# Strassen products in half of an output projection: four weight tiles loaded 20 tiles ahead, their sums formed earlier, one group of products moved

## The chip, the cores and the metric

The kernel runs on one core of a Trainium2 chip. The time is the device time of one launch in microseconds (us), taken from several executions; the profile is one profiled execution. The engines are named PE (TensorE, matrix products; PEld is its weight loading), DVE (VectorE), ACT (ScalarE), POOL (GpSimd) and SP (SyncE, here the engine that issues nearly all DMAs). They run side by side, each works its own instructions strictly in order, and they wait for one another through semaphores.

## The reference

One step of a hybrid encoder layer for two groups of tokens, 256 "prompt" and 32 "sample" tokens, D = 1024, all in float32. The part that matters here is the end:

```python
mixed = sigmoid(ga) * (branch_a @ w_out_a) + sigmoid(gb) * (branch_b @ w_out_b)
return layer_norm(DN_ALPHA * x + mixed @ w_o, ln_g, ln_b)
```

Before it come one big input projection `x @ w_in`, an mLSTM recurrence (branch A, whose final states `C_prompt` are outputs too) and a sparse attention (branch B).

## The kernel before

All weights are cut into 117 tiles of 128 x 1024 numbers (512 KB), worked one after the other in the order of the table `ORDER`. Its end is: `ga` 0 (tile 93), `wa` 0 (94), `ga` 1, `wa` 1, ... `ga` 7 (107), `wa` 7 (108), then the eight tiles of `w_o` (109 to 116; `POS["wo", 0]` is 109). The first five tiles are treated apart, the others run through a loop over the slot `t`.

A float32 product is made of three faster products: each operand is split in a high part (rounded to the type fp32r, an ACT copy, `split_hi`) and the rest (a DVE subtraction, `split_lo`), and high x high, high x low and low x high are summed. `product(t)` is 24 PE instructions for a tile, 3 for each of 8 blocks of 128. In slot `t` the program lists: the load of tile `t + 9` (`load_tile`, an SP DMA into one of eight buffers `wst`), `split_lo(t + 2)` on DVE, `evac(t - 1)` (what DVE, ACT and POOL do with the finished product, which frees one of two banks `pj`), `split_hi(t + 3)` on ACT, then `product(t)` on PE, and in its middle `side()`, where other work booked with `at(slot, ...)` is listed. Nothing orders these but the listing, the queues of the engines and the waits for data and buffers. The split parts have a ring of four buffer pairs, `wh` and `wl`.

The evacuation of a `wa` tile is a chain: DVE multiplies with the gate (`sg`), DVE adds (`mB`), ACT rounds the sum to `mxh`, DVE subtracts (`mxl`); POOL copies sample's 32 tokens to `mxs`. `mxh`/`mxl` are the left operand of `mixed @ w_o`.

The output projection of the 256 prompt tokens is done in `finish()`. Its first four of eight blocks of the summed dimension (512 of 1024) use Strassen's scheme: with `mixed` cut into a11, a12, a21, a22 and the upper half of `w_o` into b11, b12, b21, b22 (one 512 KB tile each, tiles 109 to 112 in this order), seven products replace eight. Token sums s1 to s4 (`token_sums`, `token_halves`) and weight sums t1 to t4 (`weight_sum`, one DVE subtraction of 128 x 1024 each, line L1019) are formed first:

```python
first, second = {"t1": ("b12", "b11"), "t2": ("b22", "t1"), "t3": ("b22", "b12"), "t4": ("b21", "t2")}[name]
dve.tensor_tensor(lazy["sums"][name], raw_unit(first), raw_unit(second), OP.subtract)
```

`seventh(bank, s, t)` issues one such product, a group of six PE instructions of 512 columns (line L1057). `plain(bank, rows, column)` issues a group of twelve for the lower half of `w_o` (tiles 113 to 116, called w4 to w7). `unit_hi`/`unit_lo` split a unit (b.., t.. or w..); w7 and t4 have buffers of their own, `wown` and `spare`. `b11`, `b21` and `t2` are split in the last turns of the loop. The results collect in PSUM banks y11, y12, y21, y22, and y21 is read between its groups: PE adds a11 x b11, DVE takes that to `z` (`begun(0, 0, y21)`, line L1145), PE adds s2 x t2 to the same bank, DVE reads again (`begun(0, 1, y21)`), PE adds s3 x t3, DVE reads again (`added(1, 1, y21)`, line L1149). So each of these PE groups must wait until DVE has read the one before.

Sample's 32 tokens are multiplied with the unsplit weights by `sample_rows(p)` (line L1078; 64 records in the profile), on four 32-column strips of PE side by side; DVE then takes bank `p` to `zs`. At the end come the layer norm on DVE (with a power on POOL), the stores of `y` by SP, and `state_prompt(h)`: 48 PE instructions (`c`), eight ACT copies (`oc_all`) and the stores of `C_prompt`.

Of the kernel before, what the change touches and what calls it, by code (L numbers as in the profile page):

```python
# [14 lines left out]
OP = mybir.AluOpType  # L15
# [8 lines left out]
KT = D // 128  # L24
# [6 lines left out]
FIRST = 5  # L31
SEVEN = ("b11", "b21", "t2", "t1", "t3")
# [6 lines left out]
ALPHA = 2.0 ** 0.25  # L39
# [42 lines left out]
ORDER = tile_order()  # L82
NT = len(ORDER)
POS = {t: i for i, t in enumerate(ORDER)}


def ap_of(t, offset, dims):
# [4 lines left out]
def body(ctx, tc, a, o):  # L92
    nc = tc.nc
    pe, act, dve, pool, sp = nc.tensor, nc.scalar, nc.vector, nc.gpsimd, nc.sync
# [5 lines left out]
    def sb(name, shape, dt=F32, tag=None, bufs=1):  # L100
        return P.tile(shape, dt, name=name, tag=tag or name, bufs=bufs)

    def bank(name, n=512):
        return ps.tile([128, 512], F32, name=name, tag="side", bufs=6)
# [4 lines left out]
    def at(slot, fn, *args):  # L109
        jobs[slot].append((fn, args))  # L110
# [13 lines left out]
    store, lazy, masked = {}, {}, []  # L124
    stage = {}
# [4 lines left out]
    def load_tile(t):  # L130
        if t >= NT or t in loaded:
            return
        loaded.add(t)
        stage[t] = sb(f"wst{t}", [128, KT * 128], tag="wst", bufs=8)
        sp.dma_start(stage[t], a["w"][:, t - FIRST])

    def pair(name):
# [10 lines left out]
    def unit_hi(u, home=None):  # L148
        if home is None:
            home = pair("_" + u)  # L150
        split[u] = home
        act.copy(split[u][0], raw_unit(u))

    def unit_lo(u):
        wh, wl = split[u]
        dve.tensor_tensor(wl, raw_unit(u), wh.bitcast(F32), OP.subtract)  # L156

    def split_hi(t):
        if t >= POS["wo", 0]:
            unit_hi(SEVEN[t - POS["wo", 0]])  # L160
            return
        if t in high:
            return
        load_tile(t)
        split[t] = pair(t)
        act.copy(split[t][0], stage[t])  # L166
        high.add(t)

    def split_lo(t):
        if t >= POS["wo", 0]:  # L170
            unit_lo(SEVEN[t - POS["wo", 0]])
            return
        wh, wl = split[t]
        dve.tensor_tensor(wl, stage[t], wh.bitcast(F32), OP.subtract)  # L174
# [22 lines left out]
    cki = early[:, 1376:1632]  # L197
    early2 = sb("early2", [8, NREL + 40], tag="vaT")
    rtab, rbt = early2[:, 0:NREL], early2[:, NREL:]
    lead = [sb(f"wst_k{k}", [128, KT * 128], tag="wst", bufs=8) for k in range(KT)]  # L200
    cut = T + SMALL
    mid = cut + 256
    sp.dma_start(lead[0][:, 0:cut], a["first"][:, 0, 0:cut])
# [9 lines left out]
    for k in range(KT):  # L213
# [14 lines left out]
        for part, cols in ((whf, slice(0, c)), (wh, slice(c, LEAD - T))):  # L228
            if cols.stop:
                own = slice(T + cols.start, T + cols.stop)  # L230
# [510 lines left out]
    homes = (("hn", "kw"), ("hn", "kw"), ("lg", "lg", "lg", "sw"), ("sw", "ba", "ba", "qs"))  # L741
# [276 lines left out]
        first, second = {"t1": ("b12", "b11"), "t2": ("b22", "t1"), "t3": ("b22", "b12"), "t4": ("b21", "t2")}[name]  # L1018
        dve.tensor_tensor(lazy["sums"][name], raw_unit(first), raw_unit(second), OP.subtract)  # L1019

    at(POS["wo", 0] - 6, token_sums)
    at(POS["wo", 0] - 4, token_halves)
    for n, back in (("t1", 4), ("t2", 2), ("t3", 2), ("t4", 1)):
        at(POS["wo", 0] - back, weight_sum, n)

    def moving(n):
        if n == "wb":
# [31 lines left out]
    def seventh(p, x, u, first=False):  # L1059
        x = standing(x)  # L1060
        w = split.pop(u)
        for k in range(2):
            group(p, [v[:, k] for v in x], w, slice(512 * k, 512 * k + 512), first and k == 0, k == 1)
# [7 lines left out]
    def sample_rows(p):  # L1071
        for k in range(KT):
            for q in range(4):
                if k < 4:
                    w, c = stage[POS["wo", 2 * (k // 2) + q // 2]], 512 * (k % 2) + 256 * (q % 2)
                else:
                    w, c = stage[POS["wo", k]], 256 * q
                pe.matmul(p[32 * q:32 * q + 32, 0:256], lhsT=lazy["mxs"][:, k], rhs=w[:, c:c + 256],  # L1078
                          start=(k == 0), stop=(k == KT - 1))
# [46 lines left out]
            sp.dma_start(lazy[n + "s"], ap_of(a["ln_gb"], D * i, [[256, 4], [0, TS], [1, 256]]))  # L1126

    at(POS["ga", 3], load_tail)
    at(POS["wo", 0] - 1, load_affine)

    def statistics(b, r, records):
        mv = sb(f"mv{b}", [128, 2])
# [6 lines left out]
    def finish():  # L1139
        z, zs, bst, bss = lazy["xn"], lazy["zs"], lazy["bst"], lazy["bss"]  # L1140
        g, be = lazy["g"], lazy["b"]

        def begun(b, c, p):
            half = slice(512 * c, 512 * c + 512)
            dve.scalar_tensor_tensor(z[:, b, half], z[:, b, half], ALPHA, p, op0=OP.mult, op1=OP.add)  # L1145

        def added(b, c, p):
            half = slice(512 * c, 512 * c + 512)
            dve.tensor_tensor(z[:, b, half], z[:, b, half], p, OP.add)  # L1149

        def recorded(b, c):
            dve.bn_stats(bst[:, b, c], z[:, b, 512 * c:512 * c + 512])

        def centred(b):
            mv, nr = statistics(b, slice(0, 128), bst[:, b].rearrange("p a b -> p (a b)"))
            dve.scalar_tensor_tensor(z[:, b], z[:, b], mv[:, 0:1], g, op0=OP.subtract, op1=OP.mult)
            return nr[:, 1:2]

        def scaled(b, rs):
            for c in (slice(0, 512), slice(512, 1024)):  # L1160
                dve.scalar_tensor_tensor(z[:, b, c], z[:, b, c], rs, be[:, c], op0=OP.mult, op1=OP.add)

        def put(c):
            c = slice(512 * c, 512 * c + 512)
            sp.dma_start(o["y"][128:256, c], z[:, 1, c])

        own = sb("wown", [128, 2, KT * 128], F32R, tag="a1")
        spare = sb("spare", [128, 2, KT * 128], F32R, tag="a3")
        lazy["oc"] = sb("oc_all", [128, AH, 2, CROW], tag="a6")
        pool.memset(lazy["oc"][:, :, :, 257:], 0.0)  # L1170
        y11, y12, y21, y22 = (bank(f"yn{i}") for i in range(4))
        p = bank("yns")

        unit_lo("t2")
        evac(POS["wo", 0] - 1, prev)
        seventh(y21, "a11", "b11", True)
        seventh(y11, "a12", "b21", True)
        unit_hi("t1")
        begun(0, 0, y21)
        unit_lo("t1")  # L1180
        seventh(y21, "s2", "t2")
        unit_hi("t3")
        unit_lo("t3")
        sample_rows(p)
        unit_hi("w4")
        begun(0, 1, y21)
        unit_lo("w4")
        unit_hi("w5")
        unit_lo("w5")
        seventh(y12, "s1", "t1", True)  # L1190
        unit_hi("w7", (own[:, 0], own[:, 1]))
        unit_lo("w7")
        seventh(y21, "s3", "t3")
        unit_hi("w6")
        r = slice(96, 128)
        dve.scalar_tensor_tensor(zs, lazy["xs"], ALPHA, p[:, 0:256], op0=OP.mult, op1=OP.add)
        begun(1, 1, y12)
        unit_lo("w6")
        added(1, 1, y21)
        plain(y11, 0, 0)  # L1200
        unit_hi("b22")
        unit_lo("b22")
        dve.bn_stats(bss[:, 3], zs)
        for q in range(3):
            dve.tensor_copy(bss[r, q], bss[32 * q:32 * q + 32, 3])
        mv, nr = statistics(2, r, bss[r].rearrange("p a b -> p (a b)"))
        for q in range(4):
            pool.tensor_copy(nr[32 * q:32 * q + 32, 0:1], mv[r, 0:1])
        for q in range(3):
            pool.tensor_copy(nr[32 * q:32 * q + 32, 1:2], nr[r, 1:2])  # L1210
        unit_hi("t4", (spare[:, 0], spare[:, 1]))
        unit_lo("t4")
        seventh(y12, "s4", "b22")
        plain(y12, 0, 1)
        added(0, 0, y11)
        recorded(0, 0)
        dve.scalar_tensor_tensor(zs, zs, nr[:, 0:1], lazy["gs"], op0=OP.subtract, op1=OP.mult)
        dve.scalar_tensor_tensor(zs, zs, nr[:, 1:2], lazy["bs"], op0=OP.mult, op1=OP.add)
        sp.dma_start(ap_of(o["y"], TP * D, [[256, 4], [D, TS], [1, 256]]), zs)
        seventh(y21, "a22", "t4")  # L1220
        plain(y21, 1, 0)
        plain(y22, 1, 1, True)
        added(0, 1, y12)
        recorded(0, 1)
        rs = centred(0)
        scaled(0, rs)
        sp.dma_start(o["y"][0:128], z[:, 0])
        begun(1, 0, y21)
        recorded(1, 0)
        added(1, 1, y22)  # L1230
        recorded(1, 1)
        rs = centred(1)
        for h in range(AH - 1):
            state_prompt(h)
        scaled(1, rs)
        for c in range(2):
            put(c)
        state_prompt(AH - 1)
# [36 lines left out]
    split_hi(FIRST + 2)  # L1275
    split_lo(FIRST + 2)
    held = {FIRST: (0, 1), FIRST + 1: (2,), FIRST + 2: (3,), FIRST + 3: (4,)}
    for t in range(FIRST, POS["wo", 0]):
        cur[0] = t
        for i in range(FIRST, t + 10):  # L1280
            load_tile(i)
        if FIRST < t <= CALM:
            evac(t - 1, prev)
        for i in held.get(t, ()):
            evac(i, first[i])
        if t < CALM:
            split_hi(t + 3)
        if t > FIRST:
            split_lo(t + 2)
        if t > CALM:  # L1290
            evac(t - 1, prev)
        if t >= CALM:
            split_hi(t + 3)
        prev = product(t, side)
# [88 lines left out]
```

## Time and profile before

| | us |
|---|---|
| median of 3 runs | 417.64 (416.25 to 417.68) |
| the profiled execution, whole | 417.65 |
| its span (first to last instruction) | 415.7 |
| PE busy in the span | 407.7 (98%) |
| DVE busy | 330.2 (79%) |
| ACT busy | 220.6 (53%) |
| POOL busy | 195.1 (47%) |

Times in rows of the profile count from the start of the span. "Busy" of PE has matrix products with modelled ends, which overlap. A row of a timeline gives start, duration, engine, line, operation, output<-operands, and in brackets the idle time before it with what ended that. `yn` stands for y11 to y22, `yns` for sample's bank, `wl_b`, `wl_t`, `wl_w` for low parts of b, t and w units.

### The profile page before, as it was taken

The page shows a single profiled execution, that of the slowest core. Times are in us where ns is not written, and L with a number is a line of the kernel's source. Part 1 is how long each engine was busy: PE and PEld are TensorE (multiplying, and loading weights), DVE is VectorE, ACT ScalarE, POOL GpSimd, SP SyncE. Part 2 cuts the span into 40 slices and gives each one's busy share as a digit, 9 for nine tenths or more (in the row PEclk, how much of TensorE's full clock was granted, in tenths as well). Part 3 has the DMA queues.
Part 4 walks back from the last instruction along what each step waited for, and adds up shares of the span by engine and source line. Part 5 has one row for each costly group of instructions (what it writes and reads, how often), then busy time and mean ns, then how long its engine had stood idle before and what let it go on. Part 6 is the DMA issues. An engine that isn't in the chain of part 4 may idle for free.

```text
span 415.7 us, 8484 instructions
## 1 busy us (share of the span) xinstructions
PE 407.7 (98%) x3111; PEld 395.1 (95%) x3111; DVE 330.2 (79%) x674; ACT 220.6 (53%) x426; POOL 195.1 (47%) x448
## 2 busy tenths in 40 slices
PE   9999999999999999999999999999999999996996
PEld 7999999999999999999989999999999999995686
DVE  5879789996976878797879878997765465979785
ACT  5796564543765556666535565564443354645402
POOL 0200069981397668669500045856998571000041
PEclk9999999999999999999999999999999999999899
DMA  8977889788954854769934755446656558344005
GB/s 298 387 287 212 305 277 308 249 197 273 344 149 137 275 153 134 200 186 168 303 106 118 259 141 153 143 127 182 176 151 183 154 152 309 103 140 140 0 14 208
DMA packets 43151, 81.09 MB, mean 195 GB/s; under 512 B 20682, under 2 KB 25670, under 8 KB 42182
## 3 DMA queue, kind: packets, MB, share of 16 engines
q1 hardware_dynamic: 42390, 79.73, 61.7%
q10 hardware_dynamic: 720, 0.82, 0.5%
q8 instruction: 24, 0.39, 0.4%
q14 instruction: 17, 0.14, 0.1%
HBM read 73.38 MB, written 9.06 MB: 198 GB/s over the span
## 4 chain that ended last, share of the span: by engine, by line
PE 89%; DVE 5%; ACT 2%; issue 1%; DMA 1%; ACTq 0%; DVEq 0%
PE pj L1043 24%; PE pj L1042 24%; PE pj L1044 24%; PE yn L1057 5%; PE pj L1106 1%; DVE wl L174 1%; PE yns L1078 1%; ACT wh L166 1%; DMA wst<-in_w 1%; PE pj L1101 1%; DVE t L1019 1%; PE pj L1099 1%; DVE wl_b L156 1%; DVE mB L993 1%; DVE kx L753 1%
## 5 line engine op out<-in xcount | busy, mean ns | idle before, releaser
L1043 PE MATMUL pj<-xhl,wh 128*128 128x288 f32 x704 | 207.9, 295 | 0.0
L1042 PE MATMUL pj<-xhl,wh 128*128 128x288 f32 x704 | 207.8, 295 | 0.0
L1044 PE MATMUL pj<-xhl,wl 128*128 128x288 f32 x704 | 207.6, 295 | 0.0
L174 DVE TENSOR_TENSOR wl<-wst,wh 128x1024 fp32r<-128x1024 f32 x104 | 129.7, 1248 | 17.6 <-ACT wh L166 17.2
L1042 PEld LDWEIGHTS pj<-xhl,wh 128*128 128x128 f32 x704 | 132.7, 189 | 0.6 <-issue 0.5
L1043 PEld LDWEIGHTS pj<-xhl,wh 128*128 128x128 f32 x704 | 132.6, 188 | 0.0
L1044 PEld LDWEIGHTS pj<-xhl,wl 128*128 128x128 f32 x704 | 132.4, 188 | 0.0
L166 ACT CAST wh<-wst 128x1024 fp32r<-128x1024 f32 x104 | 109.1, 1049 | 10.7 <-PE pj L1043 5.1
L121 POOL COPY pt<-bm 32x96 f32<-32x96 f32 x128 | 48.8, 381 | 19.9 <-DVE bm L636 10.7
L121 POOL COPY kaT<-kn 32x128 f32<-32x128 f32 x64 | 30.1, 471 | 5.1 <-DVE kn L734 2.5
L121 POOL COPY vn<-qaT 32x128 f32<-32x128 f32 x64 | 29.0, 453 | 2.6
L121 POOL COPY hn<-qaT 32x128 f32<-32x128 f32 x32 | 15.5, 485 | 12.1 <-DVE qaT L710 5.6
L994 POOL COPY mxs<-mB 128x32 f32<-128x32 f32 x8 | 1.7, 210 | 38.0 <-DVE mB L993 38.0
L1042 PE MATMUL pj<-bah,wh 128*128 128x288 f32 x64 | 19.0, 297 | 0.3 <-DVE sg L992 0.3
L121 POOL COPY hn<-ht 32x128 f32<-32x128 f32 x32 | 14.7, 459 | 9.3 <-DVE ht L710 8.1
L1044 PE MATMUL pj<-bah,wl 128*128 128x288 f32 x64 | 18.9, 296 | 0.0
L1043 PE MATMUL pj<-bal,wh 128*128 128x288 f32 x64 | 18.9, 296 | 0.0
L1042 PE MATMUL pj<-bbh,wh 128*128 128x288 f32 x64 | 18.9, 295 | 0.0
L1043 PE MATMUL pj<-bbl,wh 128*128 128x288 f32 x64 | 18.9, 295 | 0.0
L1044 PE MATMUL pj<-bbh,wl 128*128 128x288 f32 x64 | 18.9, 295 | 0.0
L979 ACT ACTIVATE sg<-pj 128x288 f32<-128x288 f32 x16 | 6.5, 408 | 22.1 <-PE pj L1044 22.1
L912 ACT CAST mxh<-mB 128x288 fp32r<-128x288 f32 x8 | 3.5, 433 | 25.5 <-DVE mB L993 25.5
(510 smaller groups left out, 687.0 us busy)
## 6 DMA issues: line engine op xcount, KB each, us to landing
wst<-in_w SPq DMA_DIRECT2D x112, 512.0 KB, 4.3
wst_k<-in_first SPq DMA_DIRECT2D x5, 440.0 KB, 6.7
rscr<-rrow SPq DMA_DIRECT2D x2, 768.0 KB
out_k<-kbT SPq DMA_DIRECT2D x1, 1152.0 KB, 10.1
vrows<-vat SPq DMA_DIRECT2D x8, 144.0 KB, 1.8
stC<-in_state_C SPq DMA_DIRECT2D x1, 1028.0 KB
out_C_sample<-stC SPq DMA_DIRECT2D x1, 1028.0 KB
bm<-rscr SPq DMA_DIRECT2D x1, 1024.0 KB
```

The lines of the kernel that those rows point to most:

```text
L121: pool.tensor_copy(out(quads[k], quads[i]), turned(quads[i], quads[k]))
L156: dve.tensor_tensor(wl, raw_unit(u), wh.bitcast(F32), OP.subtract)
L166: act.copy(split[t][0], stage[t])
L174: dve.tensor_tensor(wl, stage[t], wh.bitcast(F32), OP.subtract)
L753: dve.scalar_tensor_tensor(kwl[b], k, gnat[:, b, 2, h:h + 1], kwh[b].bitcast(F32), op0=OP.mult, op1=OP.subtract)
L979: act.activation(sg, q, AF.Sigmoid)
L993: dve.tensor_tensor(mx, sg, mx, OP.add)
L1019: dve.tensor_tensor(lazy["sums"][name], raw_unit(first), raw_unit(second), OP.subtract)
L1042: pe.matmul(p[:, :T], lhsT=wh[:, c], rhs=h[:, k], start=(k == 0), stop=False)
L1043: pe.matmul(p[:, :T], lhsT=wh[:, c], rhs=l[:, k], start=False, stop=False)
L1044: pe.matmul(p[:, :T], lhsT=wl[:, c], rhs=h[:, k], start=False, stop=(k == KT - 1))
L1057: pe.matmul(p, lhsT=l, rhs=r, start=first and i == 0, stop=last and i == 2, skip_group_check=True)
```

## The change

The buffers `wst` are no longer one ring of eight: `load_plan` writes out for each slot which tile is loaded and into which of eight homes. Up to tile 97 nothing is different. In slots 89 to 92 the tiles 109 to 112 (b11, b12, b21, b22) are loaded, where 98 to 101 were; they keep four of the homes. Tiles 98 to 108 and 113 to 116 follow in slots 93 to 107 through the four other homes. The four weight sums are listed in slots 94, 96, 98 and 100 in place of 105, 107, 107 and 108. In `finish()` sample's products stand ahead of s2 x t2, and the splits and reads are listed in another order.

```diff
+WO = POS["wo", 0]
+EARLY = WO - 20
+
+def load_plan():
+    slots, homes = defaultdict(list), {}
+    for t in range(FIRST, EARLY + 9):
+        slots[max(t - 9, FIRST)].append(t)
+        homes[t] = (t - FIRST) % 8
+    for i in range(4):
+        slots[EARLY + i].append(WO + i)
+        homes[WO + i] = (EARLY + 9 + i - FIRST) % 8
+    rest = [*range(EARLY + 9, WO), *range(WO + 4, NT)]
+    for i, t in enumerate(rest):
+        slots[EARLY + 4 + i].append(t)
+        homes[t] = (EARLY + 13 + i % 4 - FIRST) % 8
+    return slots, homes
...
-        stage[t] = sb(f"wst{t}", [128, KT * 128], tag="wst", bufs=8)
+        stage[t] = sb(f"wst{t}", [128, KT * 128], tag=f"wst{HOMES[t]}")
...
-    for n, back in (("t1", 4), ("t2", 2), ("t3", 2), ("t4", 1)):
-        at(POS["wo", 0] - back, weight_sum, n)
+    for i, n in enumerate(("t1", "t2", "t3", "t4")):
+        at(EARLY + 5 + 2 * i, weight_sum, n)
...
         begun(0, 0, y21)
         unit_lo("t1")
-        seventh(y21, "s2", "t2")
+        sample_rows(p)
         unit_hi("t3")
         unit_lo("t3")
-        sample_rows(p)
         unit_hi("w4")
+        unit_lo("w4")
+        unit_hi("w7", (own[:, 0], own[:, 1]))
+        unit_lo("w7")
+        seventh(y21, "s2", "t2")
+        dve.scalar_tensor_tensor(zs, lazy["xs"], ALPHA, p[:, 0:256], op0=OP.mult, op1=OP.add)
+        dve.bn_stats(bss[:, 3], zs)
         begun(0, 1, y21)
-        unit_lo("w4")
         unit_hi("w5")
         unit_lo("w5")
         seventh(y12, "s1", "t1", True)
-        unit_hi("w7", (own[:, 0], own[:, 1]))
-        unit_lo("w7")
+        begun(1, 1, y12)
+        unit_hi("w6")
+        unit_lo("w6")
         seventh(y21, "s3", "t3")
-        unit_hi("w6")
-        r = slice(96, 128)
-        dve.scalar_tensor_tensor(zs, lazy["xs"], ALPHA, p[:, 0:256], op0=OP.mult, op1=OP.add)
-        begun(1, 1, y12)
-        unit_lo("w6")
+        unit_hi("b22")
+        unit_lo("b22")
         added(1, 1, y21)
         plain(y11, 0, 0)
-        unit_hi("b22")
-        unit_lo("b22")
-        dve.bn_stats(bss[:, 3], zs)
+        unit_hi("t4", (spare[:, 0], spare[:, 1]))
+        unit_lo("t4")
...
-        unit_hi("t4", (spare[:, 0], spare[:, 1]))
-        unit_lo("t4")
...
-        for i in range(FIRST, t + 10):
+        for i in LOADS[t]:
             load_tile(i)
```

DVE from slot 105 to the split of t2, before (`sums` is the low part of the token sums, `t_5193` holds t1 to t3, `t_5194` is t4):

```order
L1010 TENSOR_TENSOR sums<-sq,sums 128x1024
L1019 TENSOR_TENSOR t_5193<-wst_4996,wst_4963 128x1024
L174 TENSOR_TENSOR wl_5175<-wst_4921,wh_5174 128x1024
L156 TENSOR_TENSOR wl_b_5214<-wst_4963,wh_b_5213 128x1024
L992 TENSOR_TENSOR sg_5211<-pj_5216,sg_5211 128x288
L993 TENSOR_TENSOR mB<-sg_5211,mB 128x288
L913 TENSOR_TENSOR mxl<-mB,mxh 128x288
L1019 TENSOR_TENSOR t_5193<-wst_5077,t_5193 128x1024
L1019 TENSOR_TENSOR t_5193<-wst_5077,wst_4996 128x1024
L156 TENSOR_TENSOR wl_b_5250<-wst_5038,wh_b_5249 128x1024
L1019 TENSOR_TENSOR t_5194<-wst_5038,t_5193 128x1024
L156 TENSOR_TENSOR wl_t_5283<-t_5193,wh_t_5282 128x1024
```

The same stretch of DVE now (the lines are those of the changed file, 20 higher):

```order
L1030 TENSOR_TENSOR sums<-sq,sums 128x1024
L194 TENSOR_TENSOR wl_5181<-wst_5083,wh_5180 128x1024
L176 TENSOR_TENSOR wl_b_5217<-wst_4539,wh_b_5216 128x1024
L1012 TENSOR_TENSOR sg_5214<-pj_5219,sg_5214 128x288
L1013 TENSOR_TENSOR mB<-sg_5214,mB 128x288
L933 TENSOR_TENSOR mxl<-mB,mxh 128x288
L176 TENSOR_TENSOR wl_b_5253<-wst_4612,wh_b_5252 128x1024
L176 TENSOR_TENSOR wl_t_5284<-t_4745,wh_t_5283 128x1024
```

All four sums have left this stretch. They stand now in the slots of `wa` tiles, here t2 and t3 in slots 96 and 98 on DVE:

```order
L1039 TENSOR_TENSOR t_4745<-wst_4651,t_4745 128x1024
L194 TENSOR_TENSOR wl_4816<-wst_4724,wh_4815 128x1024
L1012 TENSOR_TENSOR sg_4813<-pj_4818,sg_4813 128x288
L1013 TENSOR_TENSOR mB<-sg_4813,mB 128x288
L933 TENSOR_TENSOR mxl<-mB,mxh 128x288
L194 TENSOR_TENSOR wl_4857<-wst_4764,wh_4856 128x1024
L1039 TENSOR_TENSOR t_4745<-wst_4651,wst_4575 128x1024
L194 TENSOR_TENSOR wl_4894<-wst_4810,wh_4893 128x1024
```

Each sum came between the two weight splits of a pair of tiles.

On PE in `finish()`, around the end of sample's products, now (`yn_5321` is y21, `yn_5320` is y12):

```order
L1098 MATMUL yns<-wst_5211,mxs 32x256 x4
L1098 MATMUL yns<-wst_5244,mxs 32x256 x4
L1077 MATMUL yn_5321<-wh_t_5283,sums 128x512
L1077 MATMUL yn_5321<-wl_t_5284,sums 128x512
L1077 MATMUL yn_5321<-wh_t_5283,sums 128x512 x2
```

Before, the same place on PE went on with y12, since s2 x t2 stood ahead:

```order
L1078 MATMUL yns<-wst_5208,mxs 32x256 x4
L1078 MATMUL yns<-wst_5241,mxs 32x256 x4
L1057 MATMUL yn_5320<-wh_t_5342,sums 128x512
L1057 MATMUL yn_5320<-wl_t_5343,sums 128x512
L1057 MATMUL yn_5320<-wh_t_5342,sums 128x512 x2
```

Sample's products now stand between a12 x b21 and s2 x t2.

More of the change, by code (lines that the diff above doesn't have):

```diff
@@ L84 @@
 POS = {t: i for i, t in enumerate(ORDER)}
+WO = POS["wo", 0]
[13 more added lines that the diff above has]
+    return slots, homes
+LOADS, HOMES = load_plan()
 def ap_of(t, offset, dims):
@@ L158, in split_hi @@
     def split_hi(t):
-        if t >= POS["wo", 0]:
-            unit_hi(SEVEN[t - POS["wo", 0]])
+        if t >= WO:
+            unit_hi(SEVEN[t - WO])
             return
@@ L169, in split_lo @@
     def split_lo(t):
-        if t >= POS["wo", 0]:
-            unit_lo(SEVEN[t - POS["wo", 0]])
+        if t >= WO:
+            unit_lo(SEVEN[t - WO])
             return
@@ L199, in body @@
     rtab, rbt = early2[:, 0:NREL], early2[:, NREL:]
-    lead = [sb(f"wst_k{k}", [128, KT * 128], tag="wst", bufs=8) for k in range(KT)]
+    lead = [sb(f"wst_k{k}", [128, KT * 128], tag=f"wst{k}") for k in range(KT)]
     cut = T + SMALL
@@ L1019, in weight_sum @@
         dve.tensor_tensor(lazy["sums"][name], raw_unit(first), raw_unit(second), OP.subtract)
-    at(POS["wo", 0] - 6, token_sums)
-    at(POS["wo", 0] - 4, token_halves)
-    for n, back in (("t1", 4), ("t2", 2), ("t3", 2), ("t4", 1)):
-        at(POS["wo", 0] - back, weight_sum, n)
+    at(WO - 6, token_sums)
+    at(WO - 4, token_halves)
+    for i, n in enumerate(("t1", "t2", "t3", "t4")):
+        at(EARLY + 5 + 2 * i, weight_sum, n)
     def moving(n):
@@ L1128, in body @@
     at(POS["ga", 3], load_tail)
-    at(POS["wo", 0] - 1, load_affine)
+    at(WO - 1, load_affine)
     def statistics(b, r, records):
@@ L1172, in finish @@
         p = bank("yns")
+        r = slice(96, 128)
         unit_lo("t2")
-        evac(POS["wo", 0] - 1, prev)
+        evac(WO - 1, prev)
         seventh(y21, "a11", "b11", True)
@@ L1277, in body @@
     held = {FIRST: (0, 1), FIRST + 1: (2,), FIRST + 2: (3,), FIRST + 3: (4,)}
-    for t in range(FIRST, POS["wo", 0]):
+    for t in range(FIRST, WO):
         cur[0] = t
-        for i in range(FIRST, t + 10):
+        for i in LOADS[t]:
             load_tile(i)
```

## The prediction

> **What bounds the kernel now.** I read the page's first lines, then the waits of TensorE (PE), then the timelines of PE and VectorE (DVE) at the end, and last the granted clock in the place where PE had stood.
>
> The page: span, and busy time of PE with its share and number of instructions.
>
> ```profile
> span 415.7 us, 8484 instructions
> PE 407.7 (98%) x3111; PEld 395.1 (95%) x3111; DVE 330.2 (79%) x674; ACT 220.6 (53%) x426; POOL 195.1 (47%) x448
> ```
>
> PE is the engine to save time on. The span is 415.7 us and the execution took 417.65, so 1.95 us lie around it; the median of the runs is 417.64, so I use this execution's own time. The waits of PE from 340 us on are two (total, times, longest):
>
> ```profile
> PE yn L1057 <- DVE xn L1145: 3.3, 1, 3.3
> PE pj L1042 <- DVE sg L992: 0.3, 1, 0.3
> ```
>
> The PE timeline around them (start, duration, line, output<-operands, idle time before it):
>
> ```profile
> 372.97 0.40 PE L1042 MATMUL pj<-bah,wh 128*128 128x288 f32 x1 [0.27 <-DVE sg L992]
> 376.12 0.30 PE L1044 MATMUL pj<-bah,wl 128*128 128x288 f32 x1
> 376.25 0.40 PE L1057 MATMUL yn<-wh_b,mxh 128*128 128x512 f32 x1
> 378.87 0.39 PE L1057 MATMUL yn<-wh_b,mxl 128*128 128x512 f32 x1
> 382.61 0.47 PE L1057 MATMUL yn<-wh_t,sums 128*128 128x512 f32 x1 [3.35 <-DVE xn L1145]
> 384.35 5.11 PE L1078 MATMUL yns<-wst,mxs 128*32 128x256 f32 x64
> 389.39 0.49 PE L1057 MATMUL yn<-wh_t,sums 128*128 128x512 f32 x1
> 406.21 0.28 PE L766 MATMUL c<-v1h,kx 128*128 128x258 f32 x1
> ```
>
> The last tile of products ends at 376.25, two groups of six follow, and then PE stands 3.35 us until DVE has read bank y21 (`begun(0, 0, y21)`, L1145). Why DVE is late there, its own timeline shows:
>
> ```profile
> 369.06 1.22 DVE L1019 TENSOR_TENSOR t<-wst,wst 128x1024 f32<-128x1024 f32 x1
> 374.29 1.22 DVE L1019 TENSOR_TENSOR t<-wst,t 128x1024 f32<-128x1024 f32 x1
> 375.42 1.22 DVE L1019 TENSOR_TENSOR t<-wst,wst 128x1024 f32<-128x1024 f32 x1
> 376.56 1.22 DVE L156 TENSOR_TENSOR wl_b<-wst,wh_b 128x1024 fp32r<-128x1024 f32 x1
> 377.69 1.22 DVE L1019 TENSOR_TENSOR t<-wst,t 128x1024 f32<-128x1024 f32 x1
> 379.96 0.45 DVE L992 TENSOR_TENSOR sg<-pj,sg 128x288 f32<-128x288 f32 x1
> 381.78 0.68 DVE L1145 SCALAR_TENSOR_TENSOR xn<-xn,yn 128x512 f32<-128x512 f32 x1
> ```
>
> The four weight sums (L1019) stand in one unbroken queue ahead of the last tile's evacuation (L992 at 379.96, though its product ended 3.4 us earlier). From one such instruction's start to the next is 1.13 to 1.14 us (375.42 to 376.56), so they take 4 x 1.135 = 4.54 us. The stall has a second price: the stretches of sample's products (columns: PE busy with count, weight loads, DVE, granted clock, DMA share, GB/s).
>
> ```profile
> 384.34:387.34 3.00, 2.99 (x29) 1.39 (x33) 0.00 (x0) 0.50 0.00 0
> 387.34:389.39 2.05, 2.05 (x40) 0.96 (x32) 0.00 (x0) 1.00 0.00 0
> ```
>
> After the hole the granted clock is 0.50 until 387.3. The 64 recorded products go four side by side, 16 steps: 7 steps of 0.427 us at half clock, then 9 in 2.05 us, 0.228 each.
>
> The Trainium skill, TensorE: Matmul & The Clock Gate, Part 1 ("What's actually happening"), has the clock halve after an idle window of about 3.4 us that runs freely, so that a hole of 3.35 us need not always fill one. The one trace has the drop; a run of the kernel before that escapes it would be 1.7 us shorter (417.65 - 1.7 = 415.95), near the shortest of the three times, 416.25. By the row the new kernel gains against 417.65 on every run; by the rule it gains up to 1.7 less against such runs, and its own time is the same by both.
>
> **The change, part by part.**
>
> *Sums moved to slots 94, 96, 98, 100.* Four DVE instructions, 1.14 us each, now stand ahead of the second weight split (L174) of those tiles' turn. There DVE waits on ScalarE (ACT):
>
> ```profile
> 329.55 1.23 DVE L174 TENSOR_TENSOR wl<-wst,wh 128x1024 fp32r<-128x1024 f32 x1 [2.26 <-ACT wh L166]
> 335.92 1.23 DVE L174 TENSOR_TENSOR wl<-wst,wh 128x1024 fp32r<-128x1024 f32 x1 [0.84 <-ACT wh L166]
> 342.29 1.31 DVE L174 TENSOR_TENSOR wl<-wst,wh 128x1024 fp32r<-128x1024 f32 x1 [0.91 <-ACT wh L166]
> 348.65 1.23 DVE L174 TENSOR_TENSOR wl<-wst,wh 128x1024 fp32r<-128x1024 f32 x1 [0.91 <-ACT wh L166]
> DVE sg L992 <- PE pj L1044: 2.3, 4, 0.6
> ```
>
> The last row is from the waits of DVE between 326 and 372 us. The gaps take the first sum whole and all but 0.3 us of each other. That rest is hidden too: the split is for a product two tiles later, and DVE's next wait, on PE, lasts up to 0.6 us. Cost 0; bounds: nothing below, since nobody waits for a sum there, and above 3 x 0.3 = 0.9 if every rest reached PE. I take 0.
>
> *Loads.* SyncE (SP) issues the same 112 loads in the same slots; which tile comes differs. Tiles 98 to 108 now come five slots ahead, through four buffers; a buffer is free when the split of the tile four before is done (tile 98 at 333.89 + 1.2) and wanted by ACT for tile 102 at 345.43: 10.4 us.
>
> ```profile
> 333.89 1.18 DVE L174 TENSOR_TENSOR wl<-wst,wh 128x1024 fp32r<-128x1024 f32 x1
> 345.43 1.05 ACT L166 CAST wh<-wst 128x1024 fp32r<-128x1024 f32 x1
> DMA to landing us min/median/max: 3.5/3.8/4.2
> DMA to landing us min/median/max: 3.5/4.3/9.5
> ```
>
> The landing rows are of the loads issued from 300 to 380 us, and of all 112. At 4.2 us there are 6 us to spare, also for tile 105, which comes behind the 1 MB load of `xn` in SP's queue (tile 109 did before). Cost 0; even the slowest of the whole run, 9.5, fits.
>
> *DVE without the sums.* PE's own wait of 0.27 at 372.97 goes, since the sum at 369.06 stood before that evacuation. The last tile then ends at 375.98, its last product starting at 375.85. DVE, with the splits of b21 and t2 done at about 376.1, reads a finished bank 0.43 us after its last product starts, as here (the third row is for a part below):
>
> ```profile
> 390.66 0.63 PE L1057 MATMUL yn<-wh_t,sums 128*128 128x512 f32 x2
> 391.09 0.69 DVE L1145 SCALAR_TENSOR_TENSOR xn<-xn,yn 128x512 f32<-128x512 f32 x1 [1.13 <-PE yn L1057]
> 389.54 0.42 DVE L1196 SCALAR_TENSOR_TENSOR sq<-sq,yns 128x256 f32<-128x256 f32 x1 [0.80 <-PE yns L1078]
> ```
>
> So the evacuation starts at 376.3 and `begun(0, 0)` 1.82 later (379.96 to 381.78), 378.1 to 378.7: 3.7 us sooner than before. The other 0.8 of the 4.54 has no use, because DVE now waits for PE and ACT.
>
> *PE's new order.* After two groups of six (2.85 us, to 378.83) sample's products follow, which wait only for the token copy on GpSimd behind `mB` (377.0) and the last load (issued at 370.3 behind the split of tile 108, landed by 374.5). At full clock they take 16 x 0.228 = 3.65 instead of 5.04; bounds 16 x 0.427 / 2 = 3.4 and 5.04. They cover the read of y21 to spare. Then all PE work in one run: 78 products of 0.232 us (390.66 to 406.21 holds 67) are 18.1. So 378.83 + 3.65 + 18.1 = 400.6, where `state_prompt` starts (406.21 before): 5.6 us sooner.
>
> *Does anything wait anew?* The read that sample's products used to cover, `begun(0, 1)`, is now covered by one group of six (1.40 us), and queued behind six DVE instructions: splits t1, t3, w4, w7 from 378.7 (1.135 each, to 383.2), sample's two of 0.42 to 0.45. It starts at 384.1 and ends at 384.8; PE's groups of six end at 383.88 (s2 x t2), 385.28 (s1 x t1) and 386.68 (s3 x t3), so it wants y21 again at 385.28. The margin is 0.45. Next, w5 (its buffer comes free when s2 x t2 is read, 384.1; ACT 1.04), `begun(1, 1)`, then w6 done at 388.05 (wanted by the eighth product of `plain(y11, 0, 0)`, 386.68 + 7 x 0.233 = 388.31), b22 at 389.2 (wanted after that group of twelve, at 389.70), t4 at 391 (wanted at 393.9). All fit, by 0.2 to 0.5 us. New cost 0 to 1.5 us (two misses with the queue behind them); I take 0, as each margin has its row's duration in it.
>
> *The end.* Two things end the kernel: state outputs behind PE and ACT, and `y` behind DVE.
>
> ```profile
> 395.50 0.52 DVE L1205 COPY bss<-bss 32x6 f32<-32x6 f32 x3
> 396.53 1.22 DVE L156 TENSOR_TENSOR spare<-t,spare 128x1024 fp32r<-128x1024 f32 x1
> 409.91 1.41 DVE L1161 SCALAR_TENSOR_TENSOR xn<-xn,nr,rest 128x512 f32<-128x512 f32 x2 [0.45 <-POOL nr L1136]
> 410.69 0.99 SPq L1165 DMA_DIRECT2D out_y<-xn  x2
> 412.75 0.34 ACTq L771 DMA_DIRECT2D out_C_prompt<-oc_all  x1
> 412.00:414.40 2.40, 0.16 (x2) 0.00 (x0) 0.00 (x0) 0.37 (x1) 0.00 (x0) 1.00 1.01 376
> ```
>
> State: 412.75 - 5.6 = 407.15. DVE went from the copies at 395.50 to 411.32 without a long pause, 15.8 us; t4's split now stands ahead, and in its place DVE waits for GpSimd's row factors. From 391.0 that is 406.8, only 4.6 sooner. So the last stores crowd together, and the last row has the DMA engines full (1.01, 376 GB/s). The end moves by something between 4.6 and 5.6; I take 5.2, the middle, a little to PE's side because PE's store was the last. Span 415.7 - 5.2 = 410.5; time 417.65 - 5.2 = 412.4.
>
> **The rivals.**
> 1. *PE waits anew in the end part.* For it: three margins of 0.2 to 0.5 us on a DVE that is full from 378.7 to 391. Against: each uses traced durations, and a late split moves the later ones only by the same amount. A miss of 1 to 2.5 us gives 413.4 to 414.9.
> 2. *Half clock all the same.* If PE pauses again long enough ahead of sample's products, 1.4 us there return, and the 0.34 that the six products ahead of them lost (382.61 to 384.35, 1.74 for 1.40): 414.1. Against: no pause over 0.1 us is left there.
> 3. *It does not do what it says.* Should DVE be held at 369 to 378 by something the sums hid (ACT's splits, 1.05 each, one after the other behind `mxh`), the evacuation stays near 379.5, and sample's products fill only part: about 415.5 to 417.6. Against it stands ACT's idle time there:
>
> ```profile
> 373.44 0.43 ACT L912 CAST mxh<-mB 128x288 fp32r<-128x288 f32 x1 [4.31 <-DVE mB L993]
> ```
>
> 4. *Slower: the ring of four.* A load that lands later than 10.4 us makes ACT, DVE and PE wait, once per lap of four tiles, three laps. At L us the loss is 3 x (L - 10.4); it eats the gain of 5.2 at L = 12.1 and gives 419.7 at 12.8. Against it: 4.2 at most in this stretch, 9.5 anywhere.
>
> **How the numbers follow.** The forecast (411.0 to 413.4) has 0.75; rival 1 0.14, rival 2 0.03, rival 3 0.05, rival 4 0.03. The prediction is 412.4. The range: below, the state path alone with 5.6 (412.05) and 1 us of the 1.4 by which the three runs differ (416.25 to 417.68), 411.0; above, most of rival 1, 414.6. Beyond 0.5% (2.1 us, about what a measurement can tell) faster means under 415.55: cases 1 and the forecast, 2 and a little of 3, 0.92; same 0.05; slower 0.03.
>
> **What would show it.** Right: no wait of PE over 0.5 us after 370; granted clock 1.00 throughout sample's products, which take 3.5 to 3.8 us; `begun(0, 0)` about 2.1 us after the last tile's product; first `c` product 24.6 us after the first `yn` product (30.0 before); landings of `wst` under 5 us and ACT never waiting for one. Wrong: PE waiting for L1165 or for a split (`wl_w`, `wl_b`), a clock of 0.50 after 376, or a wait of ACT on a DMA between 330 and 366.

## The result and the profile after

The changed kernel takes 411.98 us (median of 4 runs, 411.88 to 412.47) against 417.66 of the kernel before (416.25 to 419.61); the ratio is 0.9863, with a 95% interval from 0.9822 to 0.9904. The forecast was 412.4. The profiled execution took 411.89 us.

The first lines of the page after: span, and busy time of the engines.

```profile
span 410.2 us, 8482 instructions
PE 405.1 (99%) x3111; PEld 394.3 (96%) x3111; DVE 330.3 (81%) x674; ACT 220.6 (54%) x426; POOL 197.2 (48%) x448
```

PE, DVE, ACT and POOL execute as many instructions as before; the span is 5.5 us shorter. The waits of PE from 300 us on, which listed two before, list none. The PE timeline of the same places:

```profile
375.75 0.40 PE L1077 MATMUL yn<-wh_b,mxh 128*128 128x512 f32 x1
378.63 3.66 PE L1098 MATMUL yns<-wst,mxs 128*32 128x256 f32 x64
382.23 0.50 PE L1077 MATMUL yn<-wh_t,sums 128*128 128x512 f32 x1
400.48 0.28 PE L786 MATMUL c<-v1h,kx 128*128 128x258 f32 x1
```

The first group on y21 starts 0.5 us sooner than before (376.25), sample's products follow without a hole, and `state_prompt` starts at 400.48 instead of 406.21. The granted clock in sample's products (columns: PE busy, weight loads, DVE, clock, DMA share, GB/s) is full:

```profile
378.63:382.23 3.60, 3.60 (x64) 1.98 (x64) 0.00 (x0) 1.00 0.10 34
```

DVE, from the token sums to the reads of y21, in which the four sums are gone:

```profile
369.07 1.22 DVE L194 TENSOR_TENSOR wl<-wst,wh 128x1024 fp32r<-128x1024 f32 x1
370.21 1.22 DVE L176 TENSOR_TENSOR wl_b<-wst,wh_b 128x1024 fp32r<-128x1024 f32 x1
376.14 0.45 DVE L1012 TENSOR_TENSOR sg<-pj,sg 128x288 f32<-128x288 f32 x1
377.95 0.68 DVE L1165 SCALAR_TENSOR_TENSOR xn<-xn,yn 128x512 f32<-128x512 f32 x1
383.93 0.69 DVE L1165 SCALAR_TENSOR_TENSOR xn<-xn,yn 128x512 f32<-128x512 f32 x1
386.80 1.22 DVE L176 TENSOR_TENSOR wl_w<-wst,wh_w 128x1024 fp32r<-128x1024 f32 x1
```

The evacuation of the last tile (`sg`) starts 3.8 us sooner than before (379.96), the first read of y21 too (381.78). Where a sum went, in slot 96 (t2, then the split behind it, which before started at 335.92), and the landings of the loads from 300 to 380 us:

```profile
335.01 1.31 DVE L1039 TENSOR_TENSOR t<-wst,t 128x1024 f32<-128x1024 f32 x1
336.24 1.30 DVE L194 TENSOR_TENSOR wl<-wst,wh 128x1024 fp32r<-128x1024 f32 x1
337.75 0.46 DVE L1012 TENSOR_TENSOR sg<-pj,sg 128x288 f32<-128x288 f32 x1 [0.21 <-PE pj L1064]
DMA to landing us min/median/max: 3.5/3.7/3.9
```

The split comes 0.32 us later, and DVE still waits 0.21 for PE behind it: nobody is held up.

Single executions differ by up to 1.5 us before any sum was moved. So I also measure each profiled execution from a fixed point, the weight split of tile 93, about 10 us ahead of the first moved sum (327.23). Its row in the two kernels, of before and of after:

```profile
316.85 1.23 DVE L174 TENSOR_TENSOR wl<-wst,wh 128x1024 fp32r<-128x1024 f32 x1 [2.32 <-ACT wh L166]
```
```profile
316.86 1.23 DVE L194 TENSOR_TENSOR wl<-wst,wh 128x1024 fp32r<-128x1024 f32 x1 [2.33 <-ACT wh L186]
```

From there to the end of the span are 98.85 us before and 93.34 after: 5.5 less (spans are given to 0.1 us).

### The profile page after: what moved, and what is told of

It reads as the page before. It is cut to its first block, busy times and chain, and to the rows that moved or that the text cites. A ratio compares the mean times of both kernels' runs of the same rounds, so it can differ in the third digit from the quotient of the medians.

```text
span 410.2 us, 8482 instructions
## 1 busy us (share of the span) xinstructions
PE 405.1 (99%) x3111; PEld 394.3 (96%) x3111; DVE 330.3 (81%) x674; ACT 220.6 (54%) x426; POOL 197.2 (48%) x448
## 4 chain that ended last, share of the span: by engine, by line
PE 97%; DMA 1%; ACT 0%; SPq 0%; ACTq 0%; issue 0%; DVE 0%
PE pj L1063 27%; PE pj L1064 27%; PE pj L1062 27%; PE yn L1077 5%; PE pj L1126 1%; DMA wst_k<-in_first 1%; PE pj L1121 1%; PE yns L1098 1%; PE pj L1124 0%; PE ix L484 0%; PE al L640 0%; PE s L704 0%; PE av L673 0%; PE c L788 0%; PE c L786 0%; PE os L616 0%
## 5 line engine op out<-in xcount | busy, mean ns | idle before, releaser
L141 POOL COPY kaT<-kn 32x128 f32<-32x128 f32 x64 | 32.8, 513 | 5.1 <-DVE kn L754 2.5
```

What stands on the lines that cost most here:

```text
L141: pool.tensor_copy(out(quads[k], quads[i]), turned(quads[i], quads[k]))
```

## The experiments

My theory: DVE was late at the end because of the four sums, and that cost PE a hole and, behind it, the half clock; loads and the new order of the end part add almost nothing by themselves. The rivals were that the new order does the work, that the four buffers cost something that the change hides, and that the half clock belongs to sample's products. All experiments in one table; "rest" is the time from that split of tile 93 to the end of the span in the profiled execution, and "PE" is from the first product on y21 to the first `c` product. The kernel before ran again beside the experiments, 29 times beside e1 to e4 (median 417.43) and 8 times beside e5 to e7 (417.51), and their ratios are to these runs. The last column counts the runs whose mean granted clock was below 0.997, for the kernel before in these 37 runs.

| kernel | median us (runs) | ratio to before, interval | rest | PE | clock below 0.997 |
|---|---|---|---|---|---|
| before | 417.66 (416.25 to 419.61) | | 98.85 | 29.96 | 31 of 37 |
| after | 411.98 (411.88 to 412.47) | 0.9863, 0.9822 to 0.9904 | 93.34 | 24.73 | 0 of 4 |
| e1: after, end part in old order | 412.41 (411.66 to 413.15) | 0.9867, 0.9843 to 0.9892 | 93.39 | 24.96 | 0 of 5 |
| e2: after, sums late | 415.52 (414.91 to 418.53) | 0.9966, 0.9941 to 0.9991 | 96.66 | 27.66 | 5 of 12 |
| e3: before with the new loads | 417.32 (416.23 to 419.34) | 0.9994, 0.9974 to 1.0013 | 98.76 | 29.87 | 10 of 12 |
| e4: before, hole filled | 416.14 (415.70 to 416.82) | 0.9965, 0.9948 to 0.9981 | 97.29 | 28.33 | 0 of 12 |
| e5: after, t4 late | 412.94 (412.55 to 413.50) | 0.9888, 0.9867 to 0.9908 | 93.88 | 25.38 | 0 of 5 |
| e6: after, three buffers | 412.61 (411.85 to 413.04) | 0.9877, 0.9855 to 0.9899 | 93.36 | 24.74 | 0 of 4 |
| e7: after, two buffers | 415.12 (414.73 to 415.22) | 0.9936, 0.9913 to 0.9959 | 96.63 | 24.95 | 0 of 4 |

The runs of the kernel before fall in three groups: 6 with a clock of 1.00 took 416.14 to 416.53 us, 24 at 0.994 to 0.996 took 417.02 to 417.82, and 7 at 0.990 took 419.11 to 419.56. The profiled execution (0.995) is one of the middle group. Against the medians of the groups (416.29, 417.44, 419.23) the changed kernel gains 4.3, 5.5 and over 7 us; the 5.5 is the usual gain, not every run's.

**e1: is it the order of the end part?** `finish()` listed as before the change, the rest as after:

```diff
-        sample_rows(p)
+        seventh(y21, "s2", "t2")
         unit_hi("t3")
         unit_lo("t3")
+        sample_rows(p)
         unit_hi("w4")
...
```

> The changed kernel (411.98) with the end part `finish()` listed in its old order: sample's products behind s2 x t2 again; loads and weight sums stay early. Theory (the gain comes from DVE being in time; the new order of the end part adds almost nothing once it is): PE waits 0.1 us for the first read of y21 (DVE reads at 377.95 to 378.63, PE is there at 378.55), no other wait over 0.2, first c product within 0.3 us of 400.5; 411.9 to 412.4. Rival (the new order is the half that pays, since sample's products cover the reads of y21): a PE wait of 1 us or more at y21; 413.3 to 415.

The PE timeline at the former hole: the last product of a12 x b21, the first of s2 x t2, sample's products, and the first `c`:

```profile
377.87 0.39 PE L1077 MATMUL yn<-wh_b,mxl 128*128 128x512 f32 x1
378.31 0.47 PE L1077 MATMUL yn<-wh_t,sums 128*128 128x512 f32 x1
379.88 3.66 PE L1098 MATMUL yns<-wst,mxs 128*32 128x256 f32 x64
400.27 0.28 PE L786 MATMUL c<-v1h,kx 128*128 128x258 f32 x1
```

Between the first two starts are 0.44 us where a step is 0.23, so PE waits 0.2 us for the read of y21, and that is all: the rest is 93.39 against 93.34, PE's stretch 24.96 against 24.73. With DVE in time the old order is as good as the new one to 0.2 us. The sums are the only difference between e3 and e1, and they take the rest from 98.76 to 93.39.

**e2: is the order enough?** Sums back in their old slots, all else as after:

```diff
-    for i, n in enumerate(("t1", "t2", "t3", "t4")):
-        at(EARLY + 5 + 2 * i, weight_sum, n)
+    for n, back in (("t1", 4), ("t2", 2), ("t3", 2), ("t4", 1)):
+        at(WO - back, weight_sum, n)
```

> The changed kernel with the four weight sums back in slots 105, 107, 107, 108; loads early, new order of the end part kept. Theory: DVE is late again as before (first read of y21 near 381.8). Sample's products now cover that read, but the second read (begun(0, 1)) comes near 387.9 while PE wants y21 at 385.5: the stall reappears there with about 3.0 us, plus the 0.3 to 0.5 us wait ahead of the last tile. 415.2 to 415.8, or 417 if the clock halves again behind that hole. Rival (the new order alone is enough to hide the sums): 412 to 413.

A wait of PE, the second read of y21 on DVE, the PE row behind it, and the clock in the hole and after it (columns: PE busy, clock, DMA share, GB/s):

```profile
PE yn L1077 <- DVE xn L1165: 2.7, 1, 2.7
387.29 0.67 DVE L1165 SCALAR_TENSOR_TENSOR xn<-xn,yn 128x512 f32<-128x512 f32 x1
388.10 0.47 PE L1077 MATMUL yn<-wh_t,sums 128*128 128x512 f32 x1 [2.66 <-DVE xn L1165]
385.50:388.10 2.60, 0.00 (x0) 1.00 0.00 0
388.10:392.00 3.90, 3.90 (x17) 1.00 0.00 0
```

The stall has moved to the next read, as forecast, with 2.66 us for the 3.0 expected. Against the changed kernel the late sums cost 3.3 by the rest. Against the kernel before the rest is 2.2 shorter, but this execution kept the full clock, and most of the 2.2 is that: against e4, which has the old order at full clock, it is 0.6 shorter (96.66 for 97.29). The other runs of e2 show it too: seven at full clock took 414.91 to 415.68, five at 0.990 to 0.996 took 416.56 to 418.53, so the half clock can come back behind this hole as well. The gains do not add: both parts attack the same wait, and e1 has nearly all of it with the sums alone.

**e3: what do the loads cost?** The kernel before with `load_plan` only (the edits of e1 and e2 together, made to the changed kernel).

> The kernel before with nothing but the new plan of loads (w_o's first four tiles 20 tiles ahead, tiles 98 to 108 through four buffers); sums and end part as before. Theory: the plan of loads costs and brings nothing by itself: 417.3 to 417.9, landings under 5 us, no wait of ACT on a load. Rival (four buffers are short, the change gains in spite of them): 418.5 or more with ACT waiting for loads between 330 and 366 us.

Waits of PE, and landings from 300 to 380 us:

```profile
PE yn L1077 <- DVE xn L1165: 3.3, 1, 3.3
PE pj L1062 <- DVE sg L1012: 0.3, 1, 0.3
DMA to landing us min/median/max: 3.6/3.8/3.9
```

Both waits of the kernel before are there unchanged, ACT waits for no load, and the time is the same within 0.3%. The plan of loads costs and brings nothing; it makes the early sums possible.

**e4: what is the half clock worth, and whose is it?** The kernel before, with dummy products in PE's hole:

```diff
         begun(0, 0, y21)
+        for _ in range(28):
+            pe.matmul(p[:, :256], lhsT=ones[:, :128], rhs=ones, start=True, stop=True)
         unit_lo("t1")
```

> The kernel before with 28 dummy products (bf16, 256 columns, into sample's bank, overwritten later) listed on PE between a12 x b21 and s2 x t2, where PE stood 3.35 us. They take about 3.0 us of the hole; nothing else changes. Theory (the hole sets the clock to half, which costs 1.39 us in sample's products and 0.34 in s2 x t2): granted clock 1.00 throughout, 415.7 to 416.1. Rival (the half clock belongs to sample's own products, 32 columns wide): clock 0.50 there again, 417.4 to 417.9.

The dummies, and sample's products behind the hole:

```profile
379.26 3.31 PE L1181 MATMUL yns<-const-bfloat16-1.0 128*128 128x256 bf16 x28
384.32 3.66 PE L1078 MATMUL yns<-wst,mxs 128*32 128x256 f32 x64
384.32:387.91 3.59, 3.59 (x64) 1.97 (x64) 0.00 (x0) 1.00 0.02 5
```

DVE's read comes no sooner (s2 x t2 starts 6.35 us after the first product on y21, 6.36 before), but PE runs at full clock behind it: sample's products take 3.59 us instead of 5.04, and the PE stretch is 1.63 us shorter (28.33 for 29.96). So the half clock follows from the hole and costs 1.6 us in these two executions, the hole itself the rest. All twelve runs kept the full clock, and their median, 416.14, is near that of the runs of the kernel before that kept it too (416.29). It lies just above what was expected (415.7 to 416.1).

**e5: how close are the margins?** t4 back in slot 108, so that DVE is 1.13 us later from the split of t2 on:

```diff
-    for i, n in enumerate(("t1", "t2", "t3", "t4")):
+    for i, n in enumerate(("t1", "t2", "t3")):
         at(EARLY + 5 + 2 * i, weight_sum, n)
+    at(WO - 1, weight_sum, "t4")
```

> The changed kernel (411.98; profiled: DVE's second read of y21, begun(0, 1), at 383.93, PE wants the bank at 385.1) with one of the four weight sums, t4, back in slot 108, so that everything on DVE from the split of t2 on comes 1.13 us later. Theory (margins as computed, 0.5 us at that read): PE waits 0.7 to 0.8 us at the third group on y21, nowhere else; clock stays 1.00; time 412.5 to 413.0. Rival A (DVE has more slack than computed, the sums need not all move): no wait, 411.9 to 412.2. Rival B (the margins are already used up, each us on DVE is a us at the end): 413.0 to 413.3.

The second read of y21 and the PE group that waits for it:

```profile
385.26 0.67 DVE L1166 SCALAR_TENSOR_TENSOR xn<-xn,yn 128x512 f32<-128x512 f32 x1
386.08 0.47 PE L1078 MATMUL yn<-wh_t,sums 128*128 128x512 f32 x1 [0.42 <-DVE xn L1166]
```

The wait is where it was expected, and shorter: 0.42 us for 0.7 to 0.8. Measured from the split of tile 93, that read comes 0.97 us later than in the changed kernel (68.04 against 67.07). PE's stretch grows by 0.65 us (25.38 for 24.73) and the rest by 0.54: a margin of 0.3 to 0.4 us is real, and beyond it DVE's time counts in full. The median rose by 0.96, which single executions blur (this one was 0.36 us late already at tile 93).

**e6 and e7: how short may the ring of buffers be?** Three, and two, in place of four for tiles 98 to 108 (n is 3 or 2; the last tiles of `w_o` take the freed homes):

```diff
-        slots[EARLY + 4 + i].append(t)
-        homes[t] = (EARLY + 13 + i % 4 - FIRST) % 8
+        slots[t - 1 - n].append(t)
+        homes[t] = free[i % n]
```

> The changed kernel with three buffers instead of four for tiles 98 to 108 (the fourth only takes a tile of w_o at the end). The time from the freeing of a buffer to ACT's need falls from 10.4 to about 7.2 us; loads land in 3.5 to 4.7. Theory (loads have time to spare): no wait of ACT on a load, 411.7 to 412.5. Rival (the ring of four is just enough): ACT waits, over 413.

> The changed kernel with two buffers for tiles 98 to 108. The time from the freeing of a buffer to ACT's need falls to about 4.0 us, against landings of 3.5 to 4.7, and one lap of two tiles (landing 3.8, high part 1.05, low part 1.2 and their queues) is about as long as PE's 6.4 us for two tiles. Theory: ACT now waits up to 1 us for loads, most behind the 1 MB load of xn near 342 us; PE's three tiles of lead cover a part, the rest makes DVE late at the end part: 412.3 to 415. If loads played no role at all: 412.0.

With three, ACT waits for no load, the rest is 93.36 and PE's stretch 24.74, both as with four; the median is 0.6 us higher, 0.1 above what was expected, and the profiled execution was 0.88 us late already at tile 93. With two, waits of ACT and of PE, the longest of ACT's, and the landings:

```profile
ACT wh L191 <- DMA wst<-in_w: 5.2, 5, 3.3
PE pj L1067 <- DVE sg L1017: 1.7, 4, 0.8
350.96 1.05 ACT L191 CAST wh<-wst 128x1024 fp32r<-128x1024 f32 x1 [3.35 <-DMA wst<-in_w]
DMA to landing us min/median/max: 3.6/4.5/6.5
```

ACT waits 5.2 us in all, 3.35 of them for one load behind the 1 MB load of `xn`, and PE then waits for late evacuations ahead of the end part; the rest is 3.3 us longer. The time, 415.12, is 0.1 above the range that was expected. So the shortened ring is a real danger, but four buffers are two away from it.

## Why the prediction was right, point by point

- *The place and its two prices.* Right. The hole of 3.35 us and PE's short wait ahead of the last tile are gone, and the half clock with them. e4 gives the clock 1.63 us; the prediction had 1.39 in sample's products and 0.34 in the six ahead, 1.73.
- *Sums hidden in slots 94 to 100.* Right: the splits behind three of them come 0.2 to 0.4 us later and nothing follows from it.
- *Loads.* Right, by e3, and by e6 with a margin that the forecast had put at 6 us. Rival 4 named the mechanism that e7 then showed, but its formula counted the load only, the same in every lap; in e7 a load behind `xn` landed after 6.5 us, ACT waited 0.8 and 3.35 us around it and under 0.5 in later laps, and PE lost its time at five late evacuations.
- *DVE in the end part.* Right to 0.2 us: evacuation at 376.14 (forecast 376.3, behind PE; in the trace DVE's own queue was busy until then), first read of y21 at 377.95 (378.1), second at 383.93 (384.1), w6 done at 388.02 (388.05). The margin of w6, 0.26 in the forecast, was used up: PE's loading of its weights waited 0.18 for it, and the product behind that one started 0.03 late. Rival 1 stood closer than its price suggests: e5 shows that one more instruction of 1.13 us on DVE brings a wait, of 0.42 us.

```profile
388.07 0.19 PEld L1077 LDWEIGHTS yn<-wl_w,mxh 128*128 128x128 f32 x1 [0.18 <-DVE wl_w L176]
```

- *PE's new order.* The sum was right: `c` starts 24.73 us after the first group on y21 (forecast 24.6), sample's products take 3.60 (3.65). But the order itself earns only 0.05 us of the rest and 0.23 of PE's stretch (e1 against after). The prediction gave the cover of the first read to sample's products; without them PE would have waited 0.2 us, not more.
- *The end.* The mis-sized term: the move of the end, put at 5.2 between 4.6 and 5.6, was 5.5. DVE's path to the last rows of `y` was put at 15.8 us from the copies on and took 14.85:

```profile
390.92 0.52 DVE L1227 COPY bss<-bss 32x6 f32<-32x6 f32 x3
393.56 0.49 DVE L1237 SCALAR_TENSOR_TENSOR sq<-sq,nr 128x256 f32<-128x256 f32 x1 [0.19 <-POOL nr L1230]
394.34 0.48 DVE L1238 SCALAR_TENSOR_TENSOR sq<-sq,nr 128x256 f32<-128x256 f32 x1 [0.30 <-POOL nr L1232]
404.36 1.41 DVE L1181 SCALAR_TENSOR_TENSOR xn<-xn,nr,rest 128x512 f32<-128x512 f32 x2 [0.45 <-POOL nr L1156]
```

  I had let DVE wait for GpSimd's row factors as long as the moved split takes, about 1.1 us; it waits 0.19 and 0.30, since an addition and a statistic stand between. So DVE is done with `y` 5.55 us sooner (405.77 for 411.32), and ahead of the last copy of the states (406.62): the path of PE and the states sets the end, as the upper of the two bounds had it.
- *The clock rule.* Right that a run of the kernel before can escape the half clock: 6 of the 37 runs beside the experiments did. The prediction put such a run at 415.95, 1.7 us under the profiled one; they took 416.14 to 416.53, by the medians 1.15 us under the middle group. It did not foresee the 7 runs at 0.990, 1.8 us above the middle group; none of them was profiled, so where their clock fell is open. The Trainium skill, TensorE: Matmul & The Clock Gate, Part 1 ("What's actually happening"), has the clock halve after an idle window of about 3.4 us that runs freely. The length agrees, 3.41 us in two traces (last section). That the window must be idle throughout does not agree: a hole of 3.35 us cannot fill 3.41, and in the kernel before PE had run for 1.3 of the 3.41 us ahead of the fall. Here the measurement decides.

## What to carry to other kernels

When the bound engine stands, look at what queued ahead of the instruction that releases it, not at that instruction: here four subtractions that could run 30 to 42 us sooner. Move such work to where its engine waits, and check what its operands need there (an early load, which cost nothing as long as a buffer's free time stayed well over a landing with a large load in front). Two cures for one wait do not add, so test each alone. And a hole of PE of 2.7 to 3.35 us can cost more than its own length here, but does not in every execution: read the clock of all runs, not of the profiled one only.

## What the runs showed that I had not expected

- The nine profiled executions differ by up to 1.5 us at the split of tile 93 (316.24 to 317.74), and by as much at a weight split near the start (19.45 to 20.94). Measured from tile 93 on, two kernels whose medians differ by 0.6 us (after and e6) agree within the 0.1 us to which a span is given.
- A delay of 0.97 us at DVE's second read of y21 cost 0.54 (e5), and one of 3.78 us (e2, 70.85 against 67.07 after the split of tile 93) cost 3.3: the first 0.4 to 0.5 us are free and the rest counts in full.
- The half clock does not begin with the work after the hole. The windows in which the granted clock falls and rises again, first of before, then of e3 (columns: PE busy, clock, DMA share, GB/s):

```profile
383.70:384.00 0.30, 0.30 (x3) 0.88 0.00 0
387.30:387.40 0.10, 0.10 (x8) 0.79 0.00 0
```
```profile
382.20:382.50 0.30, 0.30 (x2) 0.80 0.02 7
385.60:385.90 0.30, 0.30 (x8) 0.68 0.00 0
```

  Read as a change from 1.00 to 0.50 and back inside each window, it lasts from 383.93 to 387.34 and from 382.38 to 385.79, 3.41 us both times, but starts 1.3 us after PE resumed in the one (382.61) and 0.4 us in the other (381.98). In e3 it therefore fell on s2 x t2 more than on sample's products, and the PE stretch came out the same, 29.87 for 29.96.
- The falls of the clock lie on a grid, and this can explain why a hole halves the clock in one execution and not in another. In the kernel before the next fall comes behind the last product, at 414.65: 30.72 us after the first, nine times 3.413. The fall behind the last product of e2 is at 413.82. The windows in which these two fall, of before and of e2 (columns as above; no product runs in them):

```profile
414.60:414.70 0.10, 0.00 (x0) 0.74 0.00 0
```
```profile
413.80:414.00 0.20, 0.00 (x0) 0.55 0.00 0
```

  Counted back in steps of 3.413 us, e2 has borders at 389.93 and 386.52, and its hole (385.44 to 388.10) is cut in 1.08 and 1.58 us: no fall. In the kernel before, the step that ends with the fall at 383.93 has PE idle for 2.09 us, from 380.52 to 382.61. So in these traces 2.09 idle us within one step were enough and 1.58 were not, and a hole counts by how it lies on the grid. That the five runs of e2 with a lower clock had the hole in another place on the grid fits, but is not shown: they were not profiled.
